# Block transposes on VectorE and scattered stores for the residual's raw rows, in place of transposes on TensorE

## The chip, the core and the metric

The kernel runs on one core of a Trainium2 chip. Its engines each take their instructions in their own fixed order: TensorE (PE, with its weight loads PEld), VectorE (DVE), ScalarE (ACT), GpSimd (POOL), and SyncE (SP), which only issues transfers here. The metric is the device time of one execution in microseconds.

## The reference, cut to what matters

One decoder layer over 1024 prompt rows and 32 sample rows (8 requests of 4), 1056 columns when transposed, with D = 1024:

```python
h = rmsnorm(x, norm_mix_w)
p = h @ w_in          # q_a, k_a, v_a | u | z | a, b | g_a, g_b
o_a = sb_prompt(q_a, k_a, v_a, sb_bias)     # 8 heads of 64, weights
...                                         # z -> sigmoid(z) * cumprod(1 - sigmoid)
o_b, ssm_new = gdn_branch(...)              # gated delta rule
mix = (sigmoid(g_a) * (o_a @ w_pa) + sigmoid(g_b) * (o_b @ w_pb)) @ w_o
x = x + mix                                 # the residual: raw rows of x
hm = rmsnorm(x, norm_mlp_w)
x = x + square(relu(hm @ w_up)) @ w_down
```

The change concerns the raw x of the line `x = x + mix`, which the kernel needs transposed.

## The kernel before

All activations are held transposed, features on the 128 partitions and tokens along the row. The layer's products are made of three float32r matmuls for each pair of tiles (high by high, high by low, low by high: L137 to L139 in `dense`, and L937 and L938 for the scores). A weight is loaded from DRAM in a staging tile `ws_...` (L123, one buffer), split by ScalarE in its high part `wh_...` (L127) and by VectorE in its low part `wl_...` (L128).

The changed code runs in one stage, from about 640 to 800 us. It interleaves two kinds of work in `pipeline(0, SPLIT, fills)`. The first is attention: for a block of 128 queries TensorE makes scores `sc` (L937, L938, in PSUM banks of tag `d`, two of them), ScalarE takes their sigmoid `s` (L939), POOL masks it (L940) and makes `am` (L943), VectorE scans it to `pr` (L947) and multiplies (L948). Some blocks later TensorE transposes the weighted scores (`wt`, L111), ScalarE copies them (L959), and they meet the values in `po` (L985). Scores run four blocks ahead of the transposes (`LAG`). The second kind are the `fills`: four steps of each of five gate projections `pd_g_<job>_<step>` (L137 to L139 in `dense`, in banks of tag `f`, two of them), whose result ScalarE writes to a tile `gt` (L1042) and SyncE stores (L1044), and, at every second of the first 18 steps, one of nine calls of `residual_step(t)`, the function that is changed.

`residual_step` loads 128 rows of x (`xr`, L1049, one buffer; the ninth tile has 32 rows), transposes them by eight TensorE transposes into two `f` banks (`xrp`, L111), has ScalarE copy each bank to `xs` (L1056, one buffer in the pool `ak`) and SyncE store it (L1057) to `xT_d`, a DRAM tensor of 8 x 128 features by 1056 tokens. `xT_d` is read only by the output projection (L1253), in the stage after the next.

The order of the instructions on each engine isn't written out by hand: a scheduler sets it from a model of times when the program is built, with priority for the weight splits and the gates' results (`tc.high_priority()`) and one rule for the transposes `wt` (`tc.issue_after`). So an edit at one place can change the order of the whole stage. All transfers named here are issued by SyncE, in its order, to one hardware queue.

Of the kernel before, what the change touches and what calls it, by code (L numbers as in the profile page):

```python
# [8 lines left out]
F32 = mybir.dt.float32  # L9
# [3 lines left out]
AF = mybir.ActivationFunctionType  # L13
# [5 lines left out]
P = 128  # L19
D = 1024  # L20
# [18 lines left out]
def hybrid_step(ctx, tc, x_prompt, x_sample, cache_k, cache_v, page_table, state_conv, state_ssm,  # L39
# [5 lines left out]
    V, S_, G, PE, SY = nc.vector, nc.scalar, nc.gpsimd, nc.tensor, nc.sync  # L45

    def pool(name, bufs=1, stack=ctx, side=None, space=None):
        kw = {} if space is None else {"space": space}
        if side is not None:
            kw["side"] = side  # L50
        return stack.enter_context(tc.tile_pool(name=name, bufs=bufs, reuse_waits="tile", **kw))
# [12 lines left out]
    def dtile(name, f=False):  # L64
        if f:
            return psf.tile([P, 512], F32, tag="f", name=name)
        return psd.tile([P, 512], F32, tag="d", name=name)
# [21 lines left out]
    for t in range(9):  # L89
        xn = sp.tile([P, D], F32, tag="xn", name=f"xn{t}", bufs=7)  # L90
        n = P if t < 8 else NS
# [18 lines left out]
    def tr(out, in_, k=P):  # L110
        PE.transpose(out, in_, ident[:k, :k])  # L111
# [29 lines left out]
    def spill(name):  # L141
        if dbg is not None and name in dbg:
            return dbg[name]
        return dr.tile([KT, P, T], F32, name=name)

    xT_d, o_d, x1_d = spill("xT_d"), spill("o_d"), spill("x1_d")
# [43 lines left out]
    fk = pool("fk", stack=xctx)  # L190
    w0 = []
    for t in range(9):
        n = P if t < 8 else NS
        c0 = t * P
        xn = xns[t]
# [7 lines left out]
        for hf in range(2):  # L203
            pt = (ttile, gtile)[hf](f"xtp{t}_{hf}")
            pv = pt.rearrange("p (k c) -> p k c", k=4)
            for k in range(4):
                kk = hf * 4 + k
# [572 lines left out]
    NFT = 4  # L780
    sbb = cst.tile([P, NH], F32, name="sbb")
    nc.scalar.dma_start(sbb, sb_bias.to_broadcast([P, NH]))
    for p in range(4):
        for nm, col, keep_s in (("q", 0, qsT), ("k", 512, ksT), ("v", 1024, vsT)):
            hi = lo = f = None
            if nm != "q":
                f = fk.tile([P, T], F32, tag="ft", name=f"{nm}f{p}", bufs=NFT)
# [66 lines left out]
    for g in range(2):  # L854
# [14 lines left out]
        n = 260  # L869
# [41 lines left out]
    ak = pool("ak", 2, stack=actx, side="right")  # L911
# [134 lines left out]
    def residual_step(t):  # L1046
        n = P if t < 8 else NS
        xn = ak.tile([P, D], F32, tag="xr", name=f"xr{t}", bufs=1)
        SY.dma_start(xn[:n], x_prompt[0, t * P:(t + 1) * P, :] if t < 8 else x_sample.rearrange("s t d -> (s t) d"))  # L1049
        for hf in range(2):  # L1050
            pv = dtile(f"xrp{t}_{hf}", True).rearrange("p (k c) -> p k c", k=4)
            xs = ak.tile([P, 4, P], F32, tag="xs", name=f"xs{t}{hf}", bufs=1)
            for k in range(4):
                kk = hf * 4 + k
                tr(pv[:, k, :n], xn[:n, kk * P:(kk + 1) * P], n)
            S_.activation(xs[:, :, :n], pv[:, :, :n], AF.Copy)  # L1056
            SY.dma_start(xT_d[hf * 4:hf * 4 + 4, :, t * P:t * P + n].rearrange("k p c -> p k c"), xs[:, :, :n])  # L1057


    gjobs = [(j, b) for j in range(KT) for b in range(2)]  # L1060
# [13 lines left out]
    for x, (j, b) in enumerate(gjobs[11:]):  # L1074
        for c in range(len(CX)):
            fills.append(lambda j=j, b=b, c=c: gate_step(j, b, c))
            t = 4 * x + c
            if t % 2 == 0 and t // 2 < 9:
                fills.append(lambda t=t // 2: residual_step(t))
# [100 lines left out]
    for jp in range(4):  # L1180
        wa = load_w(wpav[:, :, jp * 256:(jp + 1) * 256], f"pa{jp}")
        for jj in range(2):
            j = 2 * jp + jj
# [413 lines left out]
    for c, tiles in enumerate(stages):  # L1597
        o, o2 = c * QN, c % 2 * QN
# [17 lines left out]
        with tc.high_priority():  # L1616
# [4 lines left out]
            for i, t in enumerate(tiles):  # L1621
                n = P if t < 8 else NS
# [6 lines left out]
        for i, t in enumerate(tiles):  # L1629
            n = P if t < 8 else NS  # L1630
# [37 lines left out]
```

## Time and profile before

| what | value |
|---|---|
| median of three runs | 1742.4 us (1741.89 to 1742.96) |
| the profiled execution | 1736.88 us, span 1735.2 us |
| granted clock, mean | 0.993 |
| TensorE busy | 1689.5 us, 97% |
| VectorE busy | 1143.6 us, 66% |
| ScalarE busy | 781.7 us, 45% |
| POOL busy | 198.2 us, 11% |
| DMA queue of SyncE | 43.0% of 16 engines' span |

The profile is one execution. Its time is 5.5 us below the median of the other runs, so differences are taken within it and then applied to the median. Busy shares are means over the whole span; what bounds a stage is read from windows of that stage. In the rows, `x` stands before a count, `out<-in` names the tiles, and a bracket such as `[6.81 <-ACT s L939]` gives the idle time ahead of an instruction and what ended it.

### The profile page before, as it was taken

How to read it: one execution, taken by the hardware profiler on the slowest of the kernel's cores; microseconds unless marked ns; L12 is line 12 of the kernel's file. 1: busy time of each engine (PE TensorE's matmuls, PEld its weight loads, DVE VectorE, ACT ScalarE, POOL GpSimd, SP SyncE). 2: the span in 40 equal slices, each digit the busy share in tenths (PEclk: the TensorE clock that was granted, in tenths of full speed). 3: DMA queues.
4: the chain of work that ended last, by engine and by line, in shares of the span. 5: the costliest groups of instructions: out<-in, count | busy, mean ns of one | idle time of the engine just before them, and what ended most of it. 6: DMA issues, size and time to landing. Idle time of an engine off the chain costs nothing.

```text
span 1735.2 us, 34777 instructions
## 1 busy us (share of the span) xinstructions
PE 1689.5 (97%) x14030; PEld 1631.0 (94%) x14030; DVE 1143.6 (66%) x2300; ACT 781.7 (45%) x1560; POOL 198.2 (11%) x243
## 2 busy tenths in 40 slices
PE   7999999999999989999999999999999999999998
PEld 6999999999998778887989999999999999999998
DVE  6665677867243317558757487887776778788843
ACT  5453434343324225545433356554445564344353
POOL 2110111110005214335200000000000000000000
PEclk9999999999999999999999999999999999999999
DMA  5132233234446576748134644545443666442321
GB/s 179 37 120 76 68 106 92 85 119 135 123 132 216 149 194 172 194 124 241 57 113 126 184 139 144 158 133 160 151 155 113 235 220 214 155 132 94 122 81 66
DMA packets 234220, 239.24 MB, mean 138 GB/s; under 512 B 22882, under 2 KB 192195, under 8 KB 234060
## 3 DMA queue, kind: packets, MB, share of 16 engines
q1 hardware_dynamic: 229110, 226.27, 43.0%
q0 software_dynamic: 3200, 10.52, 1.9%
q8 instruction: 110, 1.80, 0.4%
q10 hardware_dynamic: 1750, 0.23, 0.1%
q14 instruction: 50, 0.41, 0.1%
HBM read 163.21 MB, written 73.77 MB: 137 GB/s over the span
## 4 chain that ended last, share of the span: by engine, by line
PE 77%; DVE 6%; issue 6%; DMA 6%; POOL 3%; ACT 2%; SPq 0%; POOLq 0%; DVEq 0%; ACTq 0%
PE pu L139 6%; PE pu L137 6%; PE pu L138 6%; PE pw L139 4%; PE pw L138 4%; PE pw L137 4%; PE pd_g L137 2%; PE pd_g L139 2%; PE pd_g L138 2%; POOL am L943 2%; PE px L138 1%; PE px L137 1%; PE px L139 1%; PE pv L139 1%; PE pv L137 1%
## 5 line engine op out<-in xcount | busy, mean ns | idle before, releaser
L139 PE MATMUL pu<-Xh,ul 128*128 128x264 f32 x812 | 230.1, 284 | 0.0
L137 PE MATMUL pu<-Xh,uh 128*128 128x264 f32 x812 | 229.8, 283 | 0.3 <-ACT uh L1231 0.3
L138 PE MATMUL pu<-Xl,uh 128*128 128x264 f32 x812 | 229.7, 283 | 0.0
L137 PE MATMUL pw<-hc,w 128*128 128x264 f32 x728 | 205.9, 285 | 2.4 <-ACT w L1480 2.4
L138 PE MATMUL pw<-hc,w 128*128 128x264 f32 x728 | 206.1, 286 | 0.0
L139 PE MATMUL pw<-hc,w 128*128 128x264 f32 x728 | 201.3, 285 | 0.2 <-DVE w L1481 0.2
L137 PEld LDWEIGHTS pu<-Xh,uh 128*128 128x128 f32 x812 | 153.1, 189 | 0.5 <-ACT uh L1231 0.5
L138 PEld LDWEIGHTS pu<-Xl,uh 128*128 128x128 f32 x812 | 152.7, 188 | 0.0
L139 PEld LDWEIGHTS pu<-Xh,ul 128*128 128x128 f32 x812 | 152.0, 188 | 0.0
L137 PE MATMUL pd_g<-xh,wh_g 128*128 128x256 f32 (+1 forms) x512 | 150.4, 294 | 0.0
L139 PE MATMUL pd_g<-xh,wl_g 128*128 128x256 f32 (+1 forms) x512 | 149.1, 291 | 0.0
L138 PE MATMUL pd_g<-xl,wh_g 128*128 128x256 f32 (+1 forms) x512 | 148.7, 290 | 0.0
L137 PEld LDWEIGHTS pw<-hc,w 128*128 128x128 f32 x728 | 138.0, 190 | 2.7 <-ACT w L1480 2.6
L138 PEld LDWEIGHTS pw<-hc,w 128*128 128x128 f32 x728 | 137.3, 189 | 0.0
L139 PEld LDWEIGHTS pw<-hc,w 128*128 128x128 f32 x728 | 134.6, 188 | 0.4 <-DVE w L1481 0.4
L947 DVE TENSOR_TENSOR_SCAN pr<-am 128x127 f32<-128x127 f32 (+7 forms) x64 | 88.0, 1376 | 62.5 <-POOL am L943 62.4
L139 PEld LDWEIGHTS pd_g<-xh,wl_g 128*128 128x128 f32 x512 | 97.5, 190 | 3.1 <-issue 2.9
L137 PEld LDWEIGHTS pd_g<-xh,wh_g 128*128 128x128 f32 x512 | 97.6, 191 | 2.9 <-issue 2.1
L138 PEld LDWEIGHTS pd_g<-xl,wh_g 128*128 128x128 f32 x512 | 97.4, 190 | 1.0 <-issue 0.8
L1480 ACT ACTIVATE w<-a 128x512 fp32r<-128x512 f32 x78 | 43.4, 620 | 85.9 <-PE pw L139 77.6
L139 PE MATMUL px<-mh,wl_wo 128*128 128x264 f32 x256 | 72.3, 285 | 1.2 <-DVE wl_wo L1232 1.1
L138 PE MATMUL px<-ml,wh_wo 128*128 128x264 f32 x256 | 72.6, 285 | 0.0
(579 smaller groups left out, 5083.4 us busy)
## 6 DMA issues: line engine op xcount, KB each, us to landing
hc_d<-t SPq DMA_DIRECT2D x26, 924.0 KB, 4.2
hc<-hc_d SPq DMA_DIRECT2D x87, 264.0 KB, 3.7
a<-in_w_down_dram SPq DMA_DIRECT2D x48, 256.0 KB, 5.8
ws_g<-in_w_in_dram SPq DMA_DIRECT2D x16, 512.0 KB, 6.6
ws_wo<-in_w_o_dram SPq DMA_DIRECT2D x32, 256.0 KB, 4.4
ua<-in_w_up_dram SPq DMA_DIRECT2D x16, 512.0 KB, 4.3
ub<-in_w_up_dram SPq DMA_DIRECT2D x16, 512.0 KB, 5.9
gA_d<-gt SPq DMA_DIRECT2D x8, 528.0 KB, 6.5
```

What stands on the lines that cost most here:

```text
L137: PE.matmul(pt[:, :n], lhsT=wh[k], rhs=xh[k], start=(k == 0), stop=False)
L138: PE.matmul(pt[:, :n], lhsT=wh[k], rhs=xl[k], start=False, stop=False)
L139: PE.matmul(pt[:, :n], lhsT=wl[k], rhs=xh[k], start=False, stop=(k == nk - 1))
L943: G.tensor_scalar(am[:, :n], s[:, :n], -1.0, 1.0, op0=ALU.mult, op1=ALU.add)
L947: V.tensor_tensor_scan(pr[:, n - 1:0:-1], am_r, am_r, 1.0, op0=ALU.mult, op1=ALU.bypass)
L1480: S_.activation(tl[:, 0], src, AF.Copy)
```

## The change

A tile of x is now transposed by one VectorE instruction, which turns every 32x32 square of the tile in place and leaves the squares where they are. The store then puts them right: for each of the four groups of 32 partitions one store moves 32 partitions by 32 squares by 32 elements to the places of `xT_d` where these squares belong, in pieces of 32 elements (128 bytes). So a tile has four stores of 128 KB instead of two of 256 KB (the ninth tile one of 128 KB instead of two of 64 KB), 33 instead of 18 in all. The tile `xs` now holds the whole [128, 1024] and lies among the four buffers of tag `ft` that the gates' results `gt` use.

```diff
         xn = ak.tile([P, D], F32, tag="xr", name=f"xr{t}", bufs=1)
         SY.dma_start(xn[:n], x_prompt[0, t * P:(t + 1) * P, :] if t < 8 else ...)
-        for hf in range(2):
-            pv = dtile(f"xrp{t}_{hf}", True).rearrange("p (k c) -> p k c", k=4)
-            xs = ak.tile([P, 4, P], F32, tag="xs", name=f"xs{t}{hf}", bufs=1)
-            for k in range(4):
-                kk = hf * 4 + k
-                tr(pv[:, k, :n], xn[:n, kk * P:(kk + 1) * P], n)
-            S_.activation(xs[:, :, :n], pv[:, :, :n], AF.Copy)
-            SY.dma_start(xT_d[hf * 4:hf * 4 + 4, :, t * P:t * P + n].rearrange("k p c -> p k c"), xs[:, :, :n])
+
+        xs = fk.tile([P, D], F32, tag="ft", name=f"xs{t}", bufs=NFT)
+        V.transpose(xs[:n], xn[:n])
+        for a in range(n // 32):
+            o = t * P + 32 * a
+            SY.dma_start(xT_d[:, :, o:o + 32].rearrange("k (b i) j -> i (k b) j", i=32),
+                         xs[32 * a:32 * a + 32].rearrange("i (b j) -> i b j", j=32))
```

TensorE's order changes with it. Before, at the start of the interleaving (scores of head 0, blocks 3 and 4; `xrp_0`, `xrp_1` are the two halves of the first tile; `pd_g_5_1` is the second step of a gate projection):

```order
L937 MATMUL sc_3_0_7744<-kh_7702,qs_7701 128x512
L938 MATMUL sc_3_0_7744<-kl_7703,qs_7701 128x512
L111 MATMUL xrp_0_7855<-ident,xr_7853 128x128 x4
L937 MATMUL sc_4_0_7755<-kh_7702,qs_7701 128x512
L938 MATMUL sc_4_0_7755<-kl_7703,qs_7701 128x512
L111 MATMUL xrp_1_7863<-ident,xr_7853 128x128 x4
L937 MATMUL sc_4_512_7759<-kh_7702,qs_7701 128x128
L938 MATMUL sc_4_512_7759<-kl_7703,qs_7701 128x128
L111 MATMUL wt_0_0_7770<-ident,s_0_7710 128x128
L137 MATMUL pd_g_5_1_7893<-xh_171,wh_g_5_7796 128x256
```

The first half of the tile stands between the scores of blocks 3 and 4, the second behind those of block 4, and the gate's step follows the first `wt`. After, from the same scores of block 3 on:

```order
L937 MATMUL sc_3_0_7744<-kh_7702,qs_7701 128x512
L938 MATMUL sc_3_0_7744<-kl_7703,qs_7701 128x512
L137 MATMUL pd_g_5_1_7883<-xh_171,wh_g_5_7796 128x256
L138 MATMUL pd_g_5_1_7883<-xl_172,wh_g_5_7796 128x256
L139 MATMUL pd_g_5_1_7883<-xh_171,wl_g_5_7797 128x256
```

and 24 rows on, at the end of that gate step:

```order
L138 MATMUL pd_g_5_1_7883<-xl_172,wh_g_5_7796 128x256
L139 MATMUL pd_g_5_1_7883<-xh_171,wl_g_5_7797 128x256
L937 MATMUL sc_4_0_7755<-kh_7702,qs_7701 128x512
L938 MATMUL sc_4_0_7755<-kl_7703,qs_7701 128x512
L137 MATMUL pd_g_5_2_7948<-xh_169,wh_g_5_7796 128x256
L138 MATMUL pd_g_5_2_7948<-xl_170,wh_g_5_7796 128x256
L139 MATMUL pd_g_5_2_7948<-xh_169,wl_g_5_7797 128x256
```

The gate's second step, 24 matmuls, has moved ahead of the scores of block 4, and the third step starts where the tile's second half stood.

ScalarE, at blocks 5 and 6 of head 0 (`wh_g_6` is the high part of the next gate weight but one). Before:

```order
L939 ACTIVATE s_5_7773<-sc_5_512_7778,sbb 128x256
L959 ACTIVATE wt_1_7788<-wt_1_0_7789 128x256
L1042 ACTIVATE gt_5_7793<-pd_g_5_1_7893 128x256
L1056 ACTIVATE xs_7864<-xrp_1_7863 128x512
L939 ACTIVATE s_6_7832<-sc_6_0_7833,sbb 128x512
L939 ACTIVATE s_6_7832<-sc_6_512_7837,sbb 128x384
L959 ACTIVATE wt_2_7847<-wt_2_0_7848 128x384
L987 ACTIVATE oT_7826<-po_0_7827 128x128
L1042 ACTIVATE gt_5_7793<-pd_g_5_2_7958 128x256
```

and after:

```order
L939 ACTIVATE s_5_7773<-sc_5_0_7774,sbb 128x512
L939 ACTIVATE s_5_7773<-sc_5_512_7778,sbb 128x256
L959 ACTIVATE wt_1_7788<-wt_1_0_7789 128x256
L939 ACTIVATE s_6_7832<-sc_6_0_7833,sbb 128x512
L127 ACTIVATE wh_g_6_8452<-ws_g_6_8450 128x1024
L939 ACTIVATE s_6_7832<-sc_6_512_7837,sbb 128x384
L987 ACTIVATE oT_7826<-po_0_7827 128x128
L959 ACTIVATE wt_2_7847<-wt_2_0_7848 128x384
L1042 ACTIVATE gt_5_7793<-pd_g_5_3_8064 128x288
```

The copies L1056 are gone, and the split of that next weight stands between the two parts of block 6's sigmoid; before it stood behind all the rows shown and more, 32 rows after the split before it.

VectorE after the change, a little behind this place (`xs` rows are the transposes of the second and third tile):

```order
L1052 STREAM_TRANSPOSE xs_7998<-xr_7996 128x1024
L948 TENSOR_TENSOR s_4_7754<-s_4_7754,pr_4_7766 128x639
L947 SCALAR_TENSOR_TENSOR pr_5_7785<-am_5_7783 128x767
L948 TENSOR_TENSOR s_5_7773<-s_5_7773,pr_5_7785 128x767
L128 TENSOR_TENSOR wl_g_6_8453<-ws_g_6_8450,wh_g_6_8452 128x1024
L947 SCALAR_TENSOR_TENSOR pr_6_7844<-am_6_7842 128x895
L1052 STREAM_TRANSPOSE xs_8184<-xr_8182 128x1024
L948 TENSOR_TENSOR s_6_7832<-s_6_7832,pr_6_7844 128x895
```

Each transpose of a tile stands between a block's scan and its product, with the low part of the weight between them.

SyncE, from the store of a gate's result (L1044) on. Before:

```order
L1044 DMA gA_d<-gt_5_7587 128x1056
L123 DMA ws_g_6_8490<-in_w_in_dram 128x8x128
L1049 DMA xr_8006<-in_x_prompt_dram 128x1024
L1057 DMA xT_d<-xs_7856 128x4x128
L1057 DMA xT_d<-xs_7864 128x4x128
L924 DMA kh_8333<-kh_d 64x1024
L923 DMA qs_8332<-qh_d 64x1024
L925 DMA kl_8334<-kl_d 64x1024
```

and after:

```order
L1044 DMA gA_d<-gt_5_7587 128x1056
L1055 DMA xT_d<-xs_7855 32x32x32 x4
L1049 DMA xr_7996<-in_x_prompt_dram 128x1024
L123 DMA ws_g_6_8450<-in_w_in_dram 128x8x128
L1055 DMA xT_d<-xs_7998 32x32x32 x4
L1049 DMA xr_8182<-in_x_prompt_dram 128x1024
L1044 DMA gB_d<-gt_5_7793 128x1056
```

The four stores of the first tile and the load of the second tile now stand ahead of the weight's load.

## The prediction

> **What bounds the kernel now.** I read the busy times first, then the matmul waits over the whole span, then the stretch in which the changed code runs (620 to 860 us), in windows.
>
> ```profile
> span 1735.2 us, 34777 instructions
> PE 1689.5 (97%) x14030; PEld 1631.0 (94%) x14030; DVE 1143.6 (66%) x2300; ACT 781.7 (45%) x1560; POOL 198.2 (11%) x243
> ```
>
> TensorE is busy for 97% of the span, so a matmul that goes is worth its issue time, unless it fills a hole. Whether the changed stretch looks the same is told by the windows; their columns are the stretch, its length, PE, PEld, DVE, ACT and POOL busy with counts, the granted clock, the DMA share, GB/s.
>
> ```profile
> 620.00:660.00 40.00, 33.19 (x242) 31.64 (x242) 13.37 (x15) 11.76 (x26) 9.66 (x14) 0.91 0.79 200
> 660.00:700.00 40.00, 40.00 (x338) 35.56 (x337) 28.19 (x27) 23.27 (x51) 18.04 (x25) 1.00 0.75 186
> 700.00:740.00 40.00, 40.00 (x333) 35.85 (x334) 23.67 (x22) 23.33 (x51) 12.10 (x20) 1.00 0.71 190
> 740.00:780.00 40.00, 40.00 (x329) 35.26 (x326) 20.24 (x19) 20.27 (x46) 13.43 (x18) 1.00 0.48 122
> 780.00:820.00 40.00, 36.80 (x276) 29.98 (x275) 35.10 (x35) 23.13 (x46) 23.45 (x22) 1.00 0.91 262
> ```
>
> From 660 to 780 TensorE never stops. There are two holes: about 7 us before 660 and 3 us after 780 (36.80 of 40). The first is named by TensorE's and ScalarE's timelines and by the chain of waits:
>
> ```profile
> 640.00 0.60 PE L111 MATMUL xrp<-ident,xr 128*128 128x128 f32 x4
> 647.41 0.80 PE L937 MATMUL sc<-kh,qs 128*128 128x512 f32 x1 [6.81 <-ACT s L939]
> 645.83 1.06 ACT L127 ACTIVATE wh_g<-ws_g 128x1024 fp32r<-128x1024 f32 x1 [8.62 <-DMA ws_g<-in_w_in_dram]
> ...
> 633.47 12.27 DMA ws_g<-in_w_in_dram
> ```
>
> ScalarE stands in front of a gate weight (`wh_g`, L127) whose load lands at 645.74; behind it in ScalarE's order is the sigmoid `s` that would free the score bank, so TensorE waits 6.8 us. The clock suffers too:
>
> ```profile
> 644.00:648.00 4.00, 0.59 (x1) 0.50 (x2) 1.08 (x1) 2.17 (x4) 0.57 (x1) 0.67 0.56 222
> 648.00:652.00 4.00, 4.00 (x20) 3.79 (x19) 3.10 (x4) 1.89 (x5) 3.74 (x6) 0.50 0.75 165
> ```
>
> The granted clock is 0.50 right behind the hole, so work there costs double.
>
> **What the change removes.** 72 TensorE transposes and 18 ScalarE copies:
>
> ```profile
> L111 PE MATMUL xrp<-ident,xr x72: 220/272/421, 640.0 to 764.5; 128*128 128x128 f32 x64, 32*128 32x32 f32 x8
> L1056 ACT ACTIVATE xs<-xrp x18: 267/598/615, 648.1 to 765.8; 128x512 f32<-128x512 f32 x16, 128x128 f32<-128x128 f32 x2
> ...
> 648.63 0.85 PE xrp L111 x4
> 660.59 0.22 PE xrp L111 x2
> 662.07 0.81 PE xrp L111 x6
> ```
>
> The 272 ns of the first row is one record's length with its pipeline; the price of a removed matmul is its step in the chain (the last three rows): at half clock 0.85/4 = 0.21 us, at full clock 0.22/2 = 0.11 to 0.81/6 = 0.135. Of the 72, the four at 640.0 lie ahead of the hole and only delay its start: 0. The next four ran at half clock: 0.85 us. 56 full ones by 0.11 (the lower step) are 6.2 us. The eight 32x32 of the last tile lie between 0 and 8 x 0.11 = 0.9; I take 0.4, since their output is a quarter as wide and their load is not. Together 7.4 us (bounds 7.0 and 56 x 0.135 + 1.7 = 9.3). The ScalarE copies are worth nothing of their own: TensorE is full while they run.
>
> **What moves: the gate projection into the hole.** The `f` banks were shared by `xrp` and the gate's `pd_g`. In the new order the 24 matmuls of `pd_g_5_1` stand where the first four `xrp` stood, ahead of the block that waits; their weights are already in use and their bank is free. Their step is 0.21 us at half clock and, at full clock, 0.12:
>
> ```profile
> 650.46 0.21 PE pd_g L139
> ...
> 652.93 0.12 PE pd_g L138
> 653.17 0.12 PE pd_g L137
> ```
>
> In the hole's first microseconds the clock is full, so 24 x 0.12 = 2.9 us of work goes into the hole, whose end I leave where it is: ScalarE's and SyncE's orders up to that load do not differ. What of it counts: all, as TensorE was full after it. Bounds 0 and 2.9 (at 0, if the bank or ScalarE holds the group back).
>
> The remaining hole is 647.4 - 640.0 - 2.9 = 4.5 us, and the question is whether the clock then still halves. A hole much like it, elsewhere:
>
> ```profile
> 1376.04 0.59 PE L137 MATMUL pw<-hc,w 128*128 128x264 f32 x1 [2.40 <-ACT w L1480]
> 1376.00:1380.00 4.00, 3.96 (x21) 3.96 (x22) 3.96 (x8) 2.79 (x6) 0.00 (x0) 0.60 0.95 344
> ```
>
> There TensorE waited only 2.4 us, and the four microseconds behind ran at a granted clock of 0.60. So I expect a wait of 4.5 us to cost the clock as the 6.8 did, and take 0 from this, between 0 and -2.4 us (half of the 4.8 us of work that the chain shows at steps of 0.21, from 647.4 to 652.2).
>
> The Trainium skill ("TensorE: Matmul & The Clock Gate", section "What's actually happening") says otherwise: the clock halves after a whole idle window of about 3.4 us, and the windows run freely. By that rule a wait of 4.5 us mostly (an estimate: in some 7 of 10 positions) holds no whole window, the clock would stay, and the sum would be 2.4 us lower, 1731.0. The wait of 2.4 us at 1376, too short for such a window, and its 0.60 speak against it.
>
> **What the change adds on VectorE.** Nine block transposes of 128x1024; the same form stands elsewhere in the kernel:
>
> ```profile
> L484 DVE STREAM_TRANSPOSE U<-t x4: 1239/1246/1246, 161.2 to 426.3; 128x1024 f32<-128x1024 f32 x4
> ...
> 662.42 1.09 DVE L948 TENSOR_TENSOR s<-s,pr 128x895 f32<-128x895 f32 x1
> 674.62 0.98 ACT L959 ACTIVATE wt<-wt 128x512 f32<-128x512 f32 x2 [0.37 <-PE wt L111]
> ...
> DVE pr L947 <- POOL am L943: 55.8, 29, 11.1
> ```
>
> 9 x 1.246 = 11.2 us. VectorE waited 55.8 us (620 to 790) for POOL's `am`, and a block's weighted scores are done (663.5) several microseconds before TensorE's transposes of them are copied (674.6): that is the cover. If it were gone, each transpose would cost up to its 1.25 us, 11.2 in all. It is thin only in the last stretch, 780 to 820, where VectorE is busy 35.1 of 40 us and the second hole stands. TensorE's waits there (780 to 900):
>
> ```profile
> PE pb L138 <- DVE obl L1127: 2.1, 2, 1.7
> ```
>
> Bounds 0 and +2.5 (two transposes pushed in front of it); I take one, +1.25. A transpose also makes VectorE wait for its `xr` load, with the next scan (L947) behind it, for which the block's `wt` transposes on TensorE wait in turn; four stores and the load take 6.9 us (next part), while nine tiles share the 125 us from 640 to 764, 14 us each; I take 0 for it.
>
> **What the change adds on the queue.** 33 stores for 18, so 15 more issues on SyncE, and pieces of 128 instead of 512 bytes:
>
> ```profile
> L1057 SPq DMA_DIRECT2D xT_d<-xs x18: 359/365/447, 649.9 to 766.1; - x18
> xT_d<-xs SPq DMA_DIRECT2D x16, 256.0 KB, 3.8
> ms_d<-E SPq DMA_DIRECT2D x16, 32.0 KB, 1.7
> xr<-in_x_prompt_dram SPq DMA_DIRECT2D x8, 512.0 KB, 5.4
> ...
> 105.00:106.00 1.00, 1.00 (x10) 1.00 (x9) 0.00 (x0) 0.38 (x1) 0.00 (x0) 1.00 0.50 81
> 106.00:107.00 1.00, 1.00 (x11) 1.00 (x10) 0.00 (x0) 0.55 (x1) 0.00 (x0) 1.00 0.21 33
> 107.00:108.00 1.00, 1.00 (x10) 1.00 (x9) 0.48 (x2) 0.63 (x2) 0.00 (x0) 1.00 0.27 34
> ```
>
> Issue: 15 x 0.365 = 5.5 us of SyncE, spread over 120 us; hidden, unless a load stands behind stores that wait, which is the first rival. Transfer: the nearest row in piece size is `ms_d`, four 32-KB stores of 128-byte rows: 1024 pieces, just what one new 128-KB store has. The shares of the three windows behind its issue sum to 0.50 + 0.21 + 0.27 = 0.98 us of all 16 DMA engines, so 33 stores cost 32 us. The old stores I price by the window 660 to 700: 186 GB/s at a share of 0.75 is 248 GB/s, 256 KB take 1.06 us, and sixteen with two of a quarter 17.5. That is +15 us over the 120 us from 660, a share of 0.65 (mean of three windows) turned into 0.77. `xT_d` is read next by the output projection, long behind this stretch, so the stores themselves are late for nobody; I take 0, bounds 0 and the queue's rival below (+21). One tile's loop, four stores and the next `xr` load, is 4 x 0.36 + 5.4 = 6.9 us.
>
> The Trainium skill ("DMA: Bandwidth & Descriptors", Specifications) puts the least size for full rate at 512 bytes and has smaller writes read, modify and write back; the old pieces just meet that, the new ones do not. `ms_d` bears it out in part: 0.98 us against 0.53 for 128 KB at 248 GB/s, 1.8 times per byte. By the rows the sum stays as below; if scattered small writes pay more of that rule than `ms_d` did, it is the queue's rival, 1754.
>
> **The sum.** -7.4 (matmuls) - 2.9 (hole filled) + 1.25 (VectorE late) = -9.05 us. The profiled execution took 1736.9 us for its span of 1735.2 and would come to 1727.8; it stands 5.5 us below the median of the runs, 1742.4, and against that the forecast is 1742.4 - 9.0 = 1733.4 us.
>
> **Rivals.**
>
> *Given back at the next weight.* With `xrp` gone the gates run ahead, and the next weight, `wh_g_6`, stands in ScalarE's new order between the two halves of block 6's sigmoid; before, it began at 670.17.
>
> ```profile
> 648.17 0.38 SPq L123 DMA_DIRECT2D ws_g<-in_w_in_dram  x1
> 646.92 1.23 DVE L128 TENSOR_TENSOR wl_g<-ws_g,wh_g 128x1024 fp32r<-128x1024 f32 x1 [7.30 <-ACT wh_g L127]
> 656.21 1.19 ACT L939 ACTIVATE s<-sc,sbb 128x512 f32<-128x512 f32 x2
> 670.17 1.07 ACT L127 ACTIVATE wh_g<-ws_g 128x1024 fp32r<-128x1024 f32 x1
> ws_g<-in_w_in_dram SPq DMA_DIRECT2D x16, 512.0 KB, 6.6
> ```
>
> Its load cannot be issued before `wl_g` is done at 648.15. Behind up to four stores and an `xr` load it lands between 653 and 657; ScalarE comes to it at about 656. VectorE's `wl` of the same weight stands ahead of block 6's scan, so that one is held too. If it holds TensorE up for 3.5 us, the clock drops again and the slow work behind costs the 2.4 us of the first hole: +5.9, so 1739.3. Against it: 648.15 + 6.6 = 654.8 is in time. It counts as no change.
>
> *Slower: the small pieces fill the queue.* From 660 to 780 the DMA engines have 40 x (0.25 + 0.29 + 0.52) = 42 us free; with the 17.5 of the old stores the new ones have 60, which 0.98 a store (32 us) leaves half empty. But the pieces of `ms_d` lie side by side in DRAM, and those of `xT_d` 4224 bytes apart. At 2.5 times the price, 2.45 us, the stores take 81 us, and the loads of weights and heads behind them in the queue come 21 us late into the stretch from 780, which has a share of 0.91 and no room to give it back: -9 + 21 = +12, 1754. It decides from (60 + 9) / 33 = 2.1 us a store on.
>
> *VectorE becomes the bound.* If its cover does not hold, 9 x 1.25 = 11.2 less the 1.25 counted gives 1733.4 + 10 = 1743.4, no change. Against it: 28 of 40 us busy at most from 660 to 780.
>
> **How the numbers follow.** A measurement of this kernel tells about 0.2% (3.5 us) from no change, so faster means below 1738.9 and slower above 1745.9. The forecast's case 0.72; given back at the weight 0.11 and VectorE the bound 0.05, both "same", 0.16; the queue's case 0.12. The forecast's own range is 1728.5 (transposes at their upper price, 1.9 more, the clock kept for 2.4, VectorE not late for part of 1.25) to 1738 (no hole filled, VectorE late twice). To hold 8 in 10 it must take in the first rival with a load 2 us later still, 1741.5; left out are the queue's case and little below 1728.5.
>
> **What would show it.** No `xrp` rows; nine STREAM_TRANSPOSE of about 1.25 us in L1052; a wait of TensorE of about 4.5 us that still ends at 647, with 0.50 behind it; TensorE full from 660 to 780, and the work that began at 780 about 10 us earlier; DMA share about 0.8. Wrong: a second hole at 655 to 660 behind `wh_g` (first rival), waits on `qs`, `kh`, `kl`, `ws_g` loads with the share near 1 (second), waits of `wt` on VectorE's `s` (third).

## The result and the profile after

The changed kernel took 1733.3 us (1731.4 to 1735.3) against 1741.9 us (1739.9 to 1743.0) before, a ratio of 0.9946 with the interval 0.9933 to 0.9959. The forecast was 1733.4 us. The same kernel in another comparison (below) gave 0.9941 (0.9925 to 0.9957).

The profiled execution first: its span and busy times, the transposes in their new place, the stores' issues, and the waits of TensorE between 640 and 930 us (engine, line and tile that waited, who ended it, total us, times, longest).

```profile
span 1731.6 us, 34630 instructions
PE 1682.5 (97%) x13958; PEld 1624.7 (94%) x13958; DVE 1153.2 (67%) x2309; ACT 773.3 (45%) x1542; POOL 200.4 (12%) x243
...
L1055 SPq DMA_DIRECT2D xT_d<-xs x33: 309/563/4279, 646.6 to 742.7; - x33
L1052 DVE STREAM_TRANSPOSE xs<-xr x9: 1214/1236/1246, 645.3 to 741.4; 128x1024 f32<-128x1024 f32 x8, 32x1024 f32<-32x1024 f32 x1
...
PE sc L937 <- ACT s L939: 4.2, 1, 4.2
PE pb L138 <- DVE obl L1126: 2.8, 2, 2.3
```

The span is only 3.6 us shorter than that of before (1735.2), for medians 8.6 us apart. The reason is seen when the spans are cut where the changed stage begins and ends: the first score matmul (`sc`, L937) and the first matmul of the output projection (`px`). The start times in the rows of `sc` and `px`, of after and of a second profile of the kernel before:

```profile
L937 PE MATMUL sc<-kh,qs x96: 218/387/793, 641.7 to 870.1; 128*128 128x512 f32 x48, 128*128 128x128 f32 x16, 128*128 128x256 f32 x16, 128*128 128x384 f32 x16
L137 PE MATMUL px<-mh,wh_wo x256: 278/283/290, 929.8 to 1030.7; 128*128 128x264 f32 x128
```

```profile
L937 PE MATMUL sc<-kh,qs x96: 220/392/796, 642.3 to 880.9; 128*128 128x512 f32 x48, 128*128 128x128 f32 x16, 128*128 128x256 f32 x16, 128*128 128x384 f32 x16
L137 PE MATMUL px<-mh,wh_wo x256: 278/283/290, 942.1 to 1043.0; 128*128 128x264 f32 x128
```

In the profile of before that the prediction used, the stage began at 635.9 us and px at 935.8: 299.9 us. The second profile of before has 942.1 - 642.3 = 299.8 us (299.7 before rounding), after has 929.8 - 641.7 = 288.1. So the stage lost 11.7 us; the first profile of before had merely reached it some 6 us earlier than the other two, and how long an execution takes to reach it varies by more than that (634.6 to 650.1 us in the profiles of all kernels here). All experiments below are read by this stretch, taken before rounding, which repeats to a few tenths of a microsecond in the two kernels profiled twice (299.9 and 299.7 before, 288.1 and 288.3 after), and by their times beside it.

The windows that answer to those of before:

```profile
620.00:660.00 40.00, 35.83 (x276) 33.35 (x268) 11.42 (x14) 9.84 (x22) 5.70 (x10) 0.96 0.81 199
660.00:700.00 40.00, 40.00 (x322) 36.10 (x322) 30.60 (x28) 20.76 (x45) 15.64 (x22) 1.00 0.91 199
700.00:740.00 40.00, 40.00 (x336) 36.23 (x337) 29.73 (x30) 20.51 (x45) 17.29 (x25) 1.00 0.90 203
740.00:780.00 40.00, 39.52 (x325) 33.57 (x321) 29.80 (x29) 25.90 (x56) 18.56 (x24) 1.00 0.68 191
780.00:820.00 40.00, 37.40 (x288) 32.62 (x287) 34.36 (x35) 18.00 (x37) 17.73 (x19) 0.96 0.71 190
```

TensorE is full from 660 to 780 as before, but for 0.5 us; the hole ahead of 660 is smaller; the DMA share there went from a mean of 0.65 to 0.83; and the clock now dips in the last row, behind the wait for `obl` that has grown from 2.1 to 2.8 us. Right behind that wait, first before and then after:

```profile
794.00:798.00 4.00, 4.00 (x33) 3.73 (x34) 4.00 (x5) 0.37 (x1) 3.01 (x3) 1.00 1.08 253
```

```profile
789.00:793.00 4.00, 3.91 (x25) 3.64 (x27) 4.00 (x8) 0.00 (x0) 3.17 (x4) 0.57 1.01 291
```

### The profile page after: what moved, and what is told of

Read it like the earlier page. It is cut to its first block, busy times and chain, and to the rows that moved or that the text cites. A ratio compares the mean times of both kernels' runs of the same rounds, so it can differ in the third digit from the quotient of the medians.

```text
span 1731.6 us, 34630 instructions
## 1 busy us (share of the span) xinstructions
PE 1682.5 (97%) x13958; PEld 1624.7 (94%) x13958; DVE 1153.2 (67%) x2309; ACT 773.3 (45%) x1542; POOL 200.4 (12%) x243
## 4 chain that ended last, share of the span: by engine, by line
PE 88%; DMA 4%; DVE 4%; issue 2%; ACT 1%; SPq 0%; DVEq 0%; POOLq 0%; ACTq 0%
PE pu L139 6%; PE pu L137 6%; PE pu L138 6%; PE pw L139 5%; PE pw L138 5%; PE pw L137 5%; PE pd_g L137 3%; PE pd_g L139 3%; PE pd_g L138 3%; PE wt L111 2%; PE po L985 2%; PE pv L137 1%; PE pv L139 1%; PE pv L138 1%; PE px L138 1%
```

## The experiments

A table of all, then each in turn. "Stretch" is first px less first score, from the rows of `sc` and `px` in each profile; the ratio is to the kernel before, run beside it.

| kernel | ratio (interval) | stretch, us |
|---|---|---|
| before, two profiles | 1 | 299.9, 299.7 |
| after, two profiles | 0.9946, 0.9941 | 288.1, 288.3 |
| order of the change in the hole, transposes kept | 0.9993 (0.9979 to 1.0007) | 296.2 |
| before, each TensorE transpose twice | 1.0044 (1.0031 to 1.0057) | 308.6 |
| after, each VectorE transpose twice | 0.9937 (0.9913 to 0.9961) | 288.9 |
| after, 512-byte pieces | 0.9943 (0.9921 to 0.9965) | 287.4 |
| after, 50 small stores for 33 | 0.9948 (0.9927 to 0.9968) | 289.3 |
| after, 66 small stores for 33 | 1.0003 (0.9983 to 1.0023) | 300.2 |
| no VectorE transposes, 512-byte pieces, `xr` in `ft` | 0.9913 (0.9896 to 0.9929) | 281.9 |
| after, `xr` in `ft` | 0.9910 (0.9892 to 0.9929) | 283.5 |
| before, `xr` in `ft` | 1.0001 (0.9988 to 1.0014) | 298.9 |
| after, `xr` in `ft`, one weight loaded early | 0.9891 (0.9873 to 0.9909) | 281.9 |

A stretch can be taken apart: the time in which TensorE stands idle, half of its busy time at a granted clock of 0.50 (the loss to the clock), and the rest, which is its work at full clock. The split bears itself out: in six profiles with the change's TensorE order, or nearly that, the loss goes from 3.0 to 5.5 us and the idle time from 8.3 to 18.8, and the rest stays at 275.7 to 275.9.

| kernel | stretch, us | idle | loss to the clock | rest |
|---|---|---|---|---|
| before, two profiles | 299.9, 299.7 | 11.0, 10.6 | 2.4, 2.6 | 286.6, 286.5 |
| order of the change in the hole, transposes kept | 296.2 | 9.0 | 1.7 | 285.6 |
| before, each TensorE transpose twice | 308.6 | 10.7 | 4.5 | 293.4 |
| after, two profiles | 288.1, 288.3 | 9.1, 8.3 | 3.2, 4.2 | 275.8, 275.7 |
| after, `xr` in `ft` | 283.5 | 7.1 | 0 | 276.4 |
| after, `xr` in `ft`, one weight loaded early | 281.9 | 3.8 | 1.7 | 276.4 |

**The two kernels again.**

> The changed kernel unaltered, once more. In the two profiles shown, the stretch from the first score matmul to the first matmul px of the output projection took 299.9 us before and 288.1 us after, 11.8 less, while everything ahead of it took 5.8 us more in the profile after. Theory A (the gain is the issue time of the 72 transposes and the gate work that went into the hole): the stretch is again 287 to 289 us, and the 5.8 us ahead of it are a difference between executions that may be gone; time 1731 to 1735. Rival C (the 5.8 us belong to the change): the stretch begins at 641 to 642 us again.

> The kernel before unaltered, for a second profile: by theory A its stretch from the first score to the first px is 299 to 301 us again, with a hole of about 7 us before the scores of block 4, whatever the time ahead of it.

Both stretches came out as theory A has it, 288.3 and 299.7 us. The stage began at 640.2 us in the one and at 642.3 in the other, so the early start of the first profile of before (635.9) was that execution's own. Rival C falls.

**The order alone.** The transposes stay on TensorE, their output goes to another bank:

```diff
-            pv = dtile(f"xrp{t}_{hf}", True).rearrange("p (k c) -> p k c", k=4)
+            pv = gtile(f"xrp{t}_{hf}").rearrange("p (k c) -> p k c", k=4)
```

> The kernel before with one edit: the outputs xrp of its 72 transposes lie in the banks of tag g (which po uses) and no longer in the gate's f banks. All transposes, copies and 18 stores stay; the second gate step stands ahead of the scores of block 4 as in the change. It does the change's reordering alone. Theory A (8.4 us of the stretch is the transposes' own issue time, 2.6 us the hole filled): 2 to 4 us faster than before, 1738 to 1740, stretch 296 to 298 us, the wait of TensorE for the sigmoid 4 to 4.5 us for 6.8. Rival B (the gain is the order, and the transposes were nearly free): 7 to 9 us faster, 1733 to 1735. Rival G (po now waits for the g banks): same or slower than before.

```profile
PE sc L937 <- ACT s L939: 3.9, 1, 3.9
PE pb L138 <- DVE obl L1127: 1.8, 2, 0.9
PE pb L137 <- DVE tb L1145: 1.6, 1, 1.6
```

The wait for the sigmoid fell from 6.8 to 3.9 us as in the change, and the stretch to 296.2 us, 3.5 less than before: 1.6 to 2.0 of it idle time, 0.7 to 1.0 the clock, 1.0 other work. The time shows little of it (0.9993; the interval, 3.7 us faster to 1.2 slower, holds both no gain and the 3.5). Rival B, that the order is the whole gain, falls: from here to the change are another 8 us. The experiment is less clean than its text says, for TensorE's order is that of the change only in the hole and through the next blocks; behind them it is similar but not the same (the gate steps end behind the 106th score matmul here, behind the 102nd in the change, behind the 112th before). So the 8 us hold the transposes and that difference of order.

**The price of a transpose on TensorE.**

```diff
                 tr(pv[:, k, :n], xn[:n, kk * P:(kk + 1) * P], n)
+                tr(pv[:, k, :n], xn[:n, kk * P:(kk + 1) * P], n)
```

> The kernel before with each of the 72 transposes issued twice into the same place (order otherwise nearly as before). Theory A: 72 more by the 0.11 us of a step, less four that lie ahead of the hole, 7 to 8 us: stretch 306.5 to 308 us, 1748 to 1751. Rival B (transposes are nearly free beside the rest): stretch 300 to 302 us, 1742 to 1744.

Stretch 308.6 us, 8.9 more than 299.7 and above what theory A set, and 7.9 us more in the time (1743.8 for 1735.9 beside it). About 2 of the 8.9 are the clock, which here fell also behind later waits of 1.7 and 1.5 us:

```profile
808.00:812.00 4.00, 4.00 (x24) 3.55 (x25) 3.24 (x3) 2.21 (x5) 1.74 (x2) 0.57 0.98 383
```

The rest grew by 6.8 us, 0.095 for each of the 72. A transpose costs its issue time, also where it was added; rival B falls here too.

**The price of a transpose on VectorE.**

```diff
         V.transpose(xs[:n], xn[:n])
+        V.transpose(xs[:n], xn[:n])
```

> The changed kernel with each of the nine VectorE transposes done twice, order on TensorE and ScalarE unchanged: 11.2 us more of VectorE. Theory A (VectorE has cover, but for one transpose near 785 us): 0 to 2.5 us slower than the change, 1733 to 1736; TensorE's wait for obl longer by up to 1.25. Rival C (VectorE's transposes are on the path): 5 to 11 us slower, 1738 to 1744, with waits of wt on s.

Nine more cost 0.6 us of stretch (288.9 for 288.3) and nothing that the times show (0.9937). Even the 0.6 is not clear of the clock, whose loss differs by 1.0 us between the two profiles of the unaltered change. The cover holds.

**The size of the pieces.**

```diff
-        for a in range(n // 32):
-            o = t * P + 32 * a
-            SY.dma_start(xT_d[:, :, o:o + 32].rearrange(...), xs[32 * a:32 * a + 32].rearrange(...))
+        if t < 8:
+            for hf in range(2):
+                SY.dma_start(xT_d[hf * 4:hf * 4 + 4, :, t * P:t * P + n].rearrange("k p c -> p k c"),
+                             xs[:, hf * 512:(hf + 1) * 512].rearrange("p (k c) -> p k c", k=4))
+        else:
+            ...
```

> The changed kernel with its VectorE transposes and its order of TensorE and ScalarE as they are, but each of the first eight tiles stored by two stores in 512-byte pieces (16 stores for 32; the squares are left unturned, so the residual's values land in wrong places; the ninth tile is stored as in the change). Theory A (the small pieces are hidden): same as the change, 1733 within 2 us, stretch 287 to 289 us. Rival C (the small pieces take back part of the gain): 3 to 6 us faster than the change, stretch 282 to 285 us, and the wait for the block 6 and head loads shorter.

0.9943 and 287.4 us: the small pieces cost at most 0.9 us. The work at full clock is the same (275.8 us), and the clock did not fall behind the second hole here though the wait for `obl` is as long, so the 0.9 may be no cost of theirs at all. Rival C falls.

**More small stores.** Each store twice, and every other one twice, the second time to a tensor of its own:

```diff
             SY.dma_start(xT_d[:, :, o:o + 32].rearrange(...), xs[32 * a:32 * a + 32].rearrange(...))
+            SY.dma_start(xT2_d[:, :, o:o + 32].rearrange(...), xs[32 * a:32 * a + 32].rearrange(...))
```

> The changed kernel with each of the 33 small stores issued twice, the second time to a DRAM tensor of its own. One store costs 0.85 to 0.98 us of all DMA engines, so 28 to 32 us more in a stretch (660 to 780) that has 20 us free (shares 0.91, 0.90, 0.68). Theory A: about 10 us of transfers come late, part of it hidden: 0 to 8 us slower than the change (1733 to 1741), DMA share near 1 to 780. Rival by price (the prediction's queue case, a stop at 60 us of stores): 65 us of stores are just over it, +5. Rival H (the queue never decides here): 1733 and the same holes.

> The changed kernel with 17 of its 33 small stores issued twice (50 in all; order on TensorE and ScalarE as in the change), the second copies to a DRAM tensor of their own. With 66 stores the load of the next stage's input (ofs) came late, ScalarE waited 12.3 us for it and the stretch grew from 288.2 to 300.2 us. Theory A (the queue has slack that 33 stores do not use up, and decides only beyond it): with 15 us of transfers more in a stretch that had some 20 us free, stretch 288 to 290 us, time 1731 to 1735. Rival S (every store added costs the same): half of the 12 us, 294 us, 1736 to 1738.

With 50 stores nothing moved but 1.0 us of stretch. With 66 the whole gain of the change was gone (1.0003, stretch 300.2; 9.7 us more than the change beside it, above what its three theories set). The rows of the 66 stores: two windows, the waits of TensorE and ScalarE, and the issue of the load `ofs` with the copy behind it.

```profile
700.00:740.00 40.00, 40.00 (x337) 36.19 (x337) 25.93 (x23) 20.34 (x46) 19.40 (x21) 1.00 1.04 213
740.00:780.00 40.00, 27.71 (x221) 24.00 (x220) 28.16 (x29) 16.00 (x37) 16.01 (x19) 0.86 0.96 196
...
PE po L986 <- ACT wt L960: 10.9, 1, 10.9
...
ACT oah L1094 <- DMA ofs<-o_d: 12.3, 1, 12.3
...
773.61 0.53 SPq L1093 DMA_DIRECT2D ofs<-o_d  x1
776.85 0.23 ACT L1094 ACTIVATE oah<-ofs 128x32 fp32r<-128x32 f32 x1 [12.32 <-DMA ofs<-o_d]
```

The same load and copy in the change:

```profile
762.86 0.33 SPq L1090 DMA_DIRECT2D ofs<-o_d  x1
765.54 0.23 ACT L1091 ACTIVATE oah<-ofs 128x32 fp32r<-128x32 f32 x1 [0.71 <-DMA ofs<-o_d]
```

A single 16-KB load of the next stage (`ofs`) becomes late; ScalarE stands in front of it for 12.3 us, with the copies `wt` behind it that TensorE waits for. What is late is its issue. It was there 3.2 us after the issue, for 2.7 in the change, but SyncE issued it 10.8 us later. From 757.6 us on SyncE issued almost without a pause the last stores, the last `xr` load and the heads' loads that stand ahead of it. The loop of a tile (load `xr`, transpose, store) had become too slow: the ninth transpose began at 766.7 us, for 741.4 in the change. Whether SyncE is held up by the issuing itself or by a queue that is full (the share reaches 1.04) these runs do not separate. In kind this is the queue's rival of the prediction, loads behind stores, at its place (the entry into 780), though by a load that it did not name. It is not a slope: 1.0 us from 33 to 50 stores, 10.9 from 50 to 66; where between these it sets in was not tried. Rival S and rival H fall.

**The new work left out.** x is loaded straight into the tile that is stored, in 512-byte pieces:

```diff
-        xn = ak.tile([P, D], F32, tag="xr", name=f"xr{t}", bufs=1)
+        xn = fk.tile([P, D], F32, tag="ft", name=f"xr{t}", bufs=NFT)
...
-        xs = fk.tile([P, D], F32, tag="ft", name=f"xs{t}", bufs=NFT)
-        V.transpose(xs[:n], xn[:n])
+        xs = xn
```

> The changed kernel without the VectorE transposes and with 512-byte pieces: x is loaded into the tile that is stored (the residual is stored untransposed, so its values are wrong). It shows what the change would be worth if its new work cost nothing. Theory A: within 2 us of the change, 1731.5 to 1733.5, since the new work costs at most the 1.25 us that the prediction set for VectorE. Rival C: 4 us or more faster, below 1729.5.

0.9913 and 281.9 us: 6 us better than the change, which looked like rival C, against the two single experiments above. But this edit did a third thing: with its own buffer gone, the first load of x is issued later. SyncE's issues in the second profile of after, and in the next experiment, where x's load is moved alone (start us, us, engine, line):

```profile
630.81 0.72 SPq L1049 DMA_DIRECT2D xr<-in_x_prompt_dram  x1
637.26 0.39 SPq L123 DMA_DIRECT2D ws_g<-in_w_in_dram  x1
```

```profile
640.45 0.39 SPq L123 DMA_DIRECT2D ws_g<-in_w_in_dram  x1
645.07 0.34 SPq L1049 DMA_DIRECT2D xr<-in_x_prompt_dram  x1
```

In the change (as before it) the 512 KB of x stand in the queue ahead of the weight for which ScalarE waits. The next two runs tell whether that is what counted.

**The place of x's first load.** The change in full, and the kernel before, each with one edit:

```diff
-        xn = ak.tile([P, D], F32, tag="xr", name=f"xr{t}", bufs=1)
+        xn = fk.tile([P, D], F32, tag="ft", name=f"xr{t}", bufs=NFT)
```

> The changed kernel in full, with one edit: the tile xr lies among the four buffers of tag ft and no longer in a buffer of its own, so its first load (512 KB) is issued behind the load of the weight for which ScalarE waits, and no longer ahead of it. The kernel without VectorE's transposes and with big pieces had this edit in it too, and was some 5 us faster than the change; its stretch from the first score to the first px was 281.9 us for the change's 288.2. Theory Q (those 6 us came from the place of that load in the queue, not from the new work): stretch 282 to 284 us, the wait of TensorE for s about 2 us, no half clock at 650, time 1725 to 1728. Theory N (they came from the transposes and small pieces left out, which cost together what neither costs alone): stretch 287 to 289 us, 1731 to 1733. The attempt with the weight loaded ahead (1723.5) is then either no better than this (Q) or 5 us or more better (N).

> The kernel before with the same edit alone: xr in a buffer of tag ft, everything else (the 72 transposes, copies, 18 stores) as it is. Theory Q: ScalarE's weight lands some 2 us earlier here too, so the hole (6.5 to 7.1 us) shrinks to about 5, since no gate step stands in it: 2 to 4 us faster than before, 1738 to 1740, stretch 296 to 298. Theory N: as before, 300 us.

For the change with x's load moved, the wait and the clock right behind it:

```profile
PE sc L937 <- ACT s L939: 2.4, 1, 2.4
...
652.00:656.00 4.00, 2.84 (x22) 2.75 (x23) 2.81 (x4) 3.31 (x8) 2.64 (x4) 1.00 0.58 198
```

And the clock of the change itself, behind its hole (second profile):

```profile
652.00:656.00 4.00, 4.00 (x20) 3.90 (x20) 2.94 (x4) 1.39 (x4) 3.21 (x5) 0.50 0.90 208
```

Theory Q holds for the change: 283.5 us, 4.8 less, with a wait of 2.4 for 3.8 us and the clock at 1.00 where it was 0.50. Most of the 4.8 is the clock, of which no time is lost here, for 4.2 us in that profile of the change: 2.5 at this hole and 1.7 at the second one, which is also shorter (why, is not shown). A wait of 2.4 us does not always spare the clock (last section), so the split is that of one profile; the gain itself is in the six runs (0.9910). TensorE's order is here the same as in the run without the new work, so the 1.6 us between 283.5 and 281.9 is what VectorE's transposes and the small pieces cost together in these two profiles: theory N is true of 1.6 us at most. In the kernel before the same edit shortened the hole too (the wait 6.8 to 4.3 us), but the four transposes that had filled time ahead of it now came behind it, and the clock dropped all the same: 0.9 us of stretch and no difference in time, less than theory Q expected.

**A faster version.** The change with x's load moved and the weight of the first hole loaded ahead of the heads, into a staging tile of its own:

```diff
+    pre = ak.tile([P, 8, P], F32, tag="wst2", name="ws_pre", bufs=1)
+    SY.dma_start(pre, winv[:, :, 3592 + 6 * P:3592 + 7 * P])
     for x in range(LAG):
         stage_a(x)
```

> An attempt to beat the change: the changed kernel with the weight of gate job 6_0, on which ScalarE stands before the hole, loaded into a staging tile of its own ahead of the heads' loads (x rows are loaded into a tile of tag ft to make room). Theory A (the hole of 4.5 us and the half clock behind it, 1.5 us, come from that load alone): 4 to 6 us faster than the change, 1727 to 1730, no wait of TensorE for s at the first blocks. Rival L (the heads' loads come later by the same 512 KB, about 2 us, and the next gate weight then stands in the way): within 2 us of the change, a new hole nearby.

1723.5 us, 0.9891 of before: the fastest that ran, 19 us below the kernel before. No wait for the first sigmoid is left; the stretch is 281.9 us. Against the change with x's load moved (283.5) this is 1.6 us of stretch, and the intervals of the two overlap, so most of its gain over the change is x's load, not the early weight. The early weight took 3.3 us more of TensorE's idle time away, but half of that went back to the clock, which fell behind a wait of 1.8 us for a head's load at 810 us.

## Why the prediction was right, step by step

- **Matmuls, -7.4.** Right in kind, too small, and the largest miss. TensorE's work at full clock fell by 10.8 us, above the bound of 9.3 that the prediction gave. From the order kernel to the change it fell by 9.8 us, 0.137 for each of the 72, which is the upper step of the prediction (0.135) and not the lower one that it took; twice the transposes added only 0.095 each. So 0.11 is the step inside a row of transposes, and taking them out is worth more; what the rest is (the changes of order, or the passage from one kind of matmul to the next) is not shown.
- **The hole, -2.9.** Right in mechanism: 24 matmuls stand in it, the wait is 4.2 and 3.8 us for 6.8 and 6.2, and the hole between matmul starts is 4.5 and 4.1 us for the 4.5 worked out. Its end stayed where it was, as assumed: 11.3 and 10.9 us behind the first score, 11.5 and 11.0 before.
- **The clock, 0.** Held at the first hole: the clock falls to 0.50 behind it in both profiles, for a loss of 1.5 and 2.5 us (2.4 and 2.6 before). What it missed is the second hole: its wait grew, and 1.7 us are lost to the clock behind it in both profiles, none before. By the means of two profiles the term is +1.2 us.
- **VectorE, +1.25.** Near in size, wrong in mechanism. The wait for `obl` grew by 0.7 us, but the last transpose begins at 741.4 us and this wait at 786.8, so no transpose was pushed in front of it; and with x's load moved, all nine transposes are there and no wait for `obl` is left. What made it grow is not shown.
- **The queue, 0.** Held, at most 0.9 us. A share of 0.77 was expected from 660 to 780, 0.83 came. The loop of a tile, set at 6.9 us with four issues of 0.36, was longer, as the four issues took 2.2 to 7.8 us, but nine tiles still fit. The point at which the queue decides, set at 69 us of stores (2.1 us each), lies lower: 66 stores at the prediction's 0.98, that is 65 us, already took back everything, and by way of SyncE's issues, which the prediction had as hidden.
- **The sum.** By the split the stretch lost 10.8 us of work and about 2.0 of idle time and gave back about 1.2 to the clock: 11.6 (the mean of two, 299.8 to 288.2). The prediction had 7.4, 1.65 (2.9 less 1.25) and 0. By the times it is 8.6 and 10.1 us, with intervals from 7.1 to 11.7 and from 7.5 to 13.1. The forecast of -9.05 lies among the times and 2.5 us short of the stretch: the matmuls were 3.4 us too small, and the clock that it missed hid part of that. That the median fell on 1733.3 is luck beyond what the terms deserve.
- **The rivals.** No second hole came at 655 to 660, so the gain was not given back at `wh_g_6`; the queue's rival is real, but twice the stores away; VectorE did not become the bound.
- **A sign that was wrong.** The work that began at 780 was to come 10 us earlier. The first `pb` came 15 us earlier (788.2 to 773.2), though the stage began 5.8 us later: TensorE's order has 1031 matmuls of the stage ahead of it, for 1157 before, and the 72 transposes are only part of that difference.

## What to carry to other kernels

Where an engine is full through a stage, work taken off it is worth its issue step in the chain or more, and work given to an idle engine or to the queue is free until one load becomes late for the engine that stands in front of it, and then it costs at once; so test with more of it, not only with none, and see whether the load was late in its transfer or already in its issue. Split a gain in idle time, clock and work before matching it with the terms of a sum: here a second fall of the clock hid part of what the matmuls were worth. Cut spans at two marks around the change and compare the pieces: the first pair of profiles differed by 3.6 us in the span and by 11.8 us in the stage, and only the second number repeated. And an experiment that leaves work out may also move a load: repeat its edit on the full kernel before believing it.

## What was not expected of the hardware

The clock behind a short wait is not settled by the wait's length. TensorE's wait of 2.4 us for `w` at about 1370 us stands in all fourteen profiles; in eight of them the granted clock fell behind it, as in the profile of the prediction (0.60), and in six it did not, as in the one after:

```profile
1370.53 0.39 PE L137 MATMUL pw<-hc,w 128*128 128x264 f32 x1 [2.40 <-ACT w L1479]
1370.00:1374.00 4.00, 3.47 (x28) 3.47 (x29) 3.93 (x8) 3.44 (x7) 0.00 (x0) 1.00 0.89 329
```

All holes of 3.6 us and more lowered it, and in the changed stage waits of 1.5 and 2.3 us did so in some profiles and not in others. So the prediction's rule from one row (2.4 us halves the clock) was right for 4.5 us, and would have been a coin's toss for 2.4. The Trainium skill ("TensorE: Matmul & The Clock Gate", "What's actually happening") has windows of 3.4 us that run freely; that they run freely agrees with equal waits of 2.4 us ending either way, but that a whole idle window is needed does not.

Issuing a store of 1024 small pieces can hold SyncE: the median issue is 0.56 us for 0.36 before, and the longest 4.3 us. In the change no load behind such stores held TensorE up, which waited for a load 0.3 us at most from 640 to 930. With 66 stores one did.
